# The first modulation by streamed matmuls and the norm chains by a power on GpSimd, in a two-layer diffusion trunk on one core

## Chip, core and metric

One core of one Trainium2 chip. The metric is device time in microseconds (us) of one execution of the program; lower is better. Engines are TensorE (PE; its weight loads are listed as PEld), VectorE (DVE), ScalarE (ACT), GpSimd (POOL) and SyncE (SP, which issues the DMA transfers).

## What is computed

Two token groups pass through two layers with shared weights: 128 context tokens and 512 latent tokens, width 1024, all in float32. Each layer is half an FFN, a mixer (layer 0: a Fourier mix, layer 1: attention), and half an FFN. Each of the three takes a normed input that is scaled and shifted by a modulation, and its output is normed, gated and added to the stream. Cut to what the change touches:

```python
def _rmsnorm(x, g):
    y = x * lax.rsqrt(jnp.mean(x * x, axis=-1, keepdims=True) + RMS_EPS)
    return y * g
def _modulation(cond, w_mod, b_mod):                  # 1024 -> 9 x 1024
    m = jax.nn.silu(cond) @ w_mod + b_mod
    return m.reshape(cond.shape[0], N_MOD, D_MODEL)
def _modulated_prenorm(x, g, m, k):
    return _rmsnorm(x, g) * (1 + m[:, 3 * k + 1, None]) + m[:, 3 * k, None]
def _half_ffn(x, m, k, g_pre, g_post, w1, w2):
    h = _modulated_prenorm(x, g_pre, m, k)
    return x + 0.5 * m[:, 3 * k + 2, None] * _rmsnorm(_swiglu(h, w1, w2), g_post)
# in reference(): m_ctx from c_ctx for context tokens, m_lat from c for latent tokens
```

## The kernel before

The stream lies transposed: channels in 8 chunks of 128 partitions, 640 tokens along the free dimension, in two halves of 320 (half 1 ends with the 128 context tokens). Every product of a weight block with a half is three matmuls of 320 columns (`mm3`, L209 to L211): high part of the weight with the high part of the input, high with low, low with high. So each weight unit of 128 x 1024 that SP loads into a `raw` tile is split once: ScalarE copies the high part (L192), another engine subtracts it for the low part (L194). That engine is VectorE, except for the units 2 to 7, which go to GpSimd. `split` (L203, L204) does the same with inputs.

The first FFN starts with the blocks f = 0 and 1 together (4 weight units), then 2, then 3, for half 0; then the same for half 1: 384 such matmuls, called products here. Then come blocks computed from combinations of both halves (`w1_fast`).

Modulations: a row of 128 outputs needs one tile of 512 KB. `gemv` (L349) multiplies it on VectorE with the conditioning vector, which `wide` holds on all partitions, and sums along the row, once for each of the two conditions. The first two modulations (`idx` 0 and 1, shift and scale of the first FFN) are needed before anything else. `begin` makes 12 of their 16 tiles so, first for the latent condition (L312), and after the first half's norm once more for the context condition (L328), and 4 tiles by matmuls with the weights as stationary operand (L308). The other modulations are `background` jobs: `behind` takes them one by one between matmuls.

Norm chains: `inverse_rms` adds up squares (L414), reduces over partitions by three one-column matmuls (L424), takes the root on ScalarE (L426) and the reciprocal on VectorE (L427), spreads the result to all partitions by three matmuls (L432) and copies it (L435). An early activation with a square root (L416) makes ScalarE change its function table in time. `pre` scales and splits the normed input, `post` gates the output and adds it to the stream. Both are generators: `tick` advances a clock by the matmuls written so far and takes the next step of a half's chain when its `yield` time is due. The matmuls of a chain are tied behind the latest product (`in_turn`), so they stand in TensorE's row among the products. There are 24 chains: two halves, two norms for each of six sub-layers. Within an engine the order is set when the program is built, by a scheduler that goes by dependencies and priority (`high_priority` moves work ahead).

In attention, `attend` lists for each block of 128 queries the steps scores, scale, transposes (`turn`, L1103, through one PSUM bank) and weighted sum (`take`, L1119), and `weave` drops them between the products at an even pace.

## Time and profile before

| | before |
|---|---|
| time, median of 3 runs | 2358.12 us (2357.97 to 2360.28) |
| profiled execution | 2358.87 us, span of its trace 2357.0 us |
| TensorE matmul busy | 2291.1 us (97%) |
| VectorE busy | 1718.2 us (73%) |
| ScalarE busy | 1313.8 us (56%) |
| GpSimd busy | 46.7 us (2%) |

The span runs from the first to the last instruction; 1.9 us of the profiled execution lie around it, and that execution stands 0.75 us above the median. Matmul ends are modelled, so a busy TensorE need not run at its peak; the number of matmuls in a stretch, against a stretch without waits, says how much it loses. An idle time is put down to the instruction that released the wait.

### The profile page before, as it was taken

How to read it: one execution, taken by the hardware profiler on the slowest of the kernel's cores; microseconds unless marked ns; L12 is line 12 of the kernel's file. 1: busy time of each engine (PE TensorE's matmuls, PEld its weight loads, DVE VectorE, ACT ScalarE, POOL GpSimd, SP SyncE). 2: the span in 40 equal slices, each digit the busy share in tenths (PEclk: the TensorE clock that was granted, in tenths of full speed). 3: DMA queues.
4: the chain of work that ended last, by engine and by line, in shares of the span. 5: the costliest groups of instructions: out<-in, count | busy, mean ns of one | idle time of the engine just before them, and what ended most of it. 6: DMA issues, size and time to landing. Idle time of an engine off the chain costs nothing.

```text
span 2357.0 us, 39382 instructions
## 1 busy us (share of the span) xinstructions
PE 2291.1 (97%) x15692; PEld 2244.9 (95%) x15692; DVE 1718.2 (73%) x2968; ACT 1313.8 (56%) x2524; POOL 46.7 (2%) x50
## 2 busy tenths in 40 slices
PE   6899999999999999999999999999999999999997
PEld 5899999998999999999999999988888999999997
DVE  7788788478888878855888877377877585755553
ACT  3445555574574545557545545576777774545545
POOL 3100000000000000000000000000000000000000
PEclk9999999999999999999999999999999999999999
DMA  7144344424424343451334433323543222321241
GB/s 261 47 139 147 109 131 129 151 93 126 152 81 143 118 128 122 144 170 54 117 109 143 144 123 127 117 89 120 160 143 116 75 89 72 99 90 59 85 135 45
DMA packets 80141, 277.10 MB, mean 118 GB/s; under 512 B 8786, under 2 KB 15186, under 8 KB 79956
## 3 DMA queue, kind: packets, MB, share of 16 engines
q1 hardware_dynamic: 79684, 274.25, 36.0%
q8 instruction: 123, 2.02, 0.4%
q14 instruction: 62, 0.51, 0.1%
q10 hardware_dynamic: 272, 0.33, 0.0%
HBM read 263.00 MB, written 11.53 MB: 116 GB/s over the span
## 4 chain that ended last, share of the span: by engine, by line
PE 86%; DVE 5%; ACT 4%; DMA 2%; issue 2%; POOL 0%; SPq 0%; ACTq 0%; DVEq 0%
PE main L209 25%; PE main L211 25%; PE main L210 25%; PE score L209 2%; PE score L210 2%; PE score L211 2%; DVE junk L349 2%; ACT hi L192 1%; PE sum L1119 1%; PE turn L1103 1%; PE score L1077 1%; DVE lo L194 1%; PE sum L424 1%; DMA raw<-in_w 1%; PE sum L432 1%
## 5 line engine op out<-in xcount | busy, mean ns | idle before, releaser
L209 PE MATMUL main<-ring,hi 128*128 128x320 f32 x3872 | 1203.2, 312 | 19.2 <-ACT ring L203 18.1
L210 PE MATMUL main<-ring,hi 128*128 128x320 f32 x3872 | 1201.5, 310 | 1.6 <-DVE ring L204 1.5
L211 PE MATMUL main<-ring,lo 128*128 128x320 f32 x3872 | 1200.8, 310 | 1.7 <-POOL lo L194 1.6
L209 PEld LDWEIGHTS main<-ring,hi 128*128 128x128 f32 x3872 | 728.3, 188 | 26.2 <-ACT ring L203 20.3
L210 PEld LDWEIGHTS main<-ring,hi 128*128 128x128 f32 x3872 | 730.1, 189 | 4.2 <-DVE ring L204 3.3
L211 PEld LDWEIGHTS main<-ring,lo 128*128 128x128 f32 x3872 | 729.5, 188 | 2.5 <-POOL lo L194 2.2
L192 ACT ACTIVATE hi<-raw 128x1024 fp32r<-128x1024 f32 (+1 forms) x358 | 350.7, 982 | 471.5 <-PE main L210 382.1
L194 DVE TENSOR_TENSOR lo<-raw,hi 128x1024 fp32r<-128x1024 f32 (+1 forms) x354 | 398.1, 1125 | 160.8 <-ACT hi L192 159.7
L349 DVE SCALAR_TENSOR_TENSOR junk<-raw,wide 128x1024 bf16<-128x1024 f32 x256 | 312.6, 1221 | 18.5 <-DMA raw<-in_w_mod_t 16.1
L644 ACT ACTIVATE y<-main 128x320 f32<-128x320 f32 x320 | 137.8, 432 | 170.4 <-PE main L211 169.2
L385 DVE TENSOR_TENSOR total<-total,square 128x640 f32<-128x640 f32 x71 | 58.3, 823 | 114.5 <-ACT square L384 113.6
L632 ACT ACTIVATE main<-y 128x320 f32<-128x320 f32 x256 | 111.8, 440 | 23.5 <-DVE left L618 9.9
L209 PE MATMUL score<-ring,hi 128*128 128x320 f32 x384 | 118.8, 310 | 0.9 <-ACT ring L203 0.9
L210 PE MATMUL score<-ring,hi 128*128 128x320 f32 x384 | 118.7, 309 | 0.4 <-DVE ring L204 0.4
L211 PE MATMUL score<-ring,lo 128*128 128x320 f32 x384 | 118.6, 309 | 0.0
L194 DVE TENSOR_TENSOR lo<-sums,hi 128x1024 fp32r<-128x1024 f32 x64 | 78.2, 1222 | 51.5 <-ACT hi L192 51.5
L211 PE MATMUL main<-ring,ring 128*128 128x320 f32 x352 | 110.0, 313 | 5.8 <-POOL ring L194 5.8
L209 PE MATMUL main<-ring,ring 128*128 128x320 f32 x352 | 111.5, 318 | 0.0
L210 PE MATMUL main<-ring,ring 128*128 128x320 f32 x352 | 109.8, 312 | 0.0
L192 ACT ACTIVATE hi<-sums 128x1024 fp32r<-128x1024 f32 x64 | 67.9, 1061 | 27.9 <-PE main L210 20.5
L203 ACT ACTIVATE ring<-right 128x320 fp32r<-128x320 f32 x112 | 51.6, 468 | 46.5 <-DVE right L531 38.0
L604 DVE TENSOR_TENSOR left<-left,main 128x320 f32<-128x320 f32 x64 | 31.2, 487 | 59.6 <-PE main L211 59.6
(189 smaller groups left out, 2783.4 us busy)
## 6 DMA issues: line engine op xcount, KB each, us to landing
raw<-in_w SPq DMA_DIRECT2D x264, 512.0 KB, 3.6
raw<-in_w_mod_t SPq DMA_DIRECT2D x128, 512.0 KB, 3.6
raw<-in_qkv SPq DMA_DIRECT2D x26, 512.0 KB, 3.6
spill<-ring SPq DMA_DIRECT2D x12, 640.0 KB, 3.4
ring<-spill SPq DMA_DIRECT2D x12, 640.0 KB, 5.4
raw<-in_bias SPq DMA_DIRECT2D x16, 448.0 KB, 3.6
first<-in_w_mod_t SPq DMA_DIRECT2D x8, 512.0 KB, 10.2
raw<-in_four_in SPq DMA_DIRECT2D x8, 512.0 KB, 3.6
```

The costliest lines, as they stand in the source:

```text
L192: nc.scalar.activation(hi, raw[:, at], AF.Copy)
L194: engine.tensor_tensor(lo, raw[:, at], hi.bitcast(F32), op=ALU.subtract)
L203: self.nc.scalar.activation(hi, src, AF.Copy)
L209: mm(out, whi, xhi, start=start, stop=False)
L210: mm(out, whi, xlo, start=False, stop=False)
L211: self.latest = mm(out, wlo, xhi, start=False, stop=stop)
L349: last = self.nc.vector.scalar_tensor_tensor(out=self.junk, in0=raw, scalar=1.0, in1=self.wide[:, cond, :], op0=ALU.mult, op1=ALU.mult, ac ...
L385: nc.vector.tensor_tensor(acc, acc, sq, op=ALU.add)
L424: nc.tensor.matmul(ps[:, j : j + 1], acc[0][:, t : t + P], self.ones[:, :1], start=True, stop=True)
L604: tt(a, q, z, op=ALU.subtract)
L632: nc.scalar.activation(ps[:, :HALF], self.y[:, m, lo:hi], AF.Copy)
L644: nc.scalar.activation(self.y[:, m, lo:hi], ps[:, :HALF], AF.Copy)
```

## The change

- `begin`: all 16 tiles of the first two modulations go through TensorE, with the conditions as stationary operand (32 columns, of which 2 are used) and the weights as moving operand: four matmuls of 256 columns a tile, each to its own 32 partitions of the output. The result is copied, turned by two small matmuls each, and copied to `mod`. Scale (`idx` 1) comes first, then x of half 0, then shift (`idx` 0). All `gemv` calls of `begin` go, for both conditions.
- `wide`, which the background jobs still need, is loaded by one broadcast DMA behind x of half 1 and run through Silu after the first FFN block.
- `send`: no low parts on GpSimd. `pre`: no products with the norm on GpSimd in the first chain.
- `inverse_rms`: instead of a square root and a reciprocal, VectorE adds EPS and GpSimd raises to the power -0.5; the early table change goes; the wait before the spread is 2200 instead of 1800. Parts of `pre`, `post` and the chain get high priority.
- `attend`: the scaling of the block before comes ahead of the new scores, and `take` is a step of its own.

```diff
@@ send
-        engine = nc.gpsimd if self.sent in range(2, 8) else nc.vector
-        engine.tensor_tensor(lo, raw[:, at], hi.bitcast(F32), op=ALU.subtract)
+        nc.vector.tensor_tensor(lo, raw[:, at], hi.bitcast(F32), op=ALU.subtract)
@@ setup
+        self.conds = self.temp("right")[:, : NCH * 32].rearrange("p (k m) -> p k m", m=32)
+        nc.scalar.activation(self.conds[:, :, :2], self.sk, AF.Silu)
@@ begin
+        for idx in (1, 0):
+            out = ps[:, idx * 256 : (idx + 1) * 256]
+            for k in range(NCH):
+                raw = self.wts.tile([P, UNIT], F32, tag=("hi", "lo")[k % 2], name=self.name("first"))
+                nc.sync.dma_start(out=raw, in_=io["w_mod_k"][idx, k])
+                for j in range(4):
+                    self.latest = nc.tensor.matmul(out[32 * j : 32 * j + 32], self.conds[:, k, :],
+                                                   raw[:, j * 256 : (j + 1) * 256], start=k == 0, stop=k == NCH - 1)
+                if idx == 0 and k in (4, 6):
+                    self.step(0)
+            with self.tc.high_priority():
+                rows = self.temp("left")[:, :256]
+                nc.scalar.activation(rows, out, AF.Copy)
+                turned = self.bank("score")[:, :16]
+                for a in range(2):
+                    nc.tensor.matmul(turned[:, a * 8 : a * 8 + 8].rearrange("p (j c) -> p j c", j=4),
+                                     rows[:, a * P : (a + 1) * P], sel, start=True, stop=True)
...
-        for raw, j in late:
-            with self.tc.issue_after(self.first_low.ins):
-                self.gemv(raw, 0, j, (1,))
+        nc.sync.dma_start(out=self.wide, in_=io["cond_rows"].unsqueeze(0).to_broadcast([P, 2, D]))
+        self.later = [partial(nc.scalar.activation, self.wide, self.wide, AF.Silu)]
@@ inverse_rms
-        nc.scalar.activation(self.col(1), acc[0][:, :1] if final else spare, AF.Sqrt)
...
-        nc.scalar.activation(col, ps[:, :3], AF.Sqrt, bias=self.eps, scale=1.0 / D)
-        nc.vector.reciprocal(col, col)
-        yield 1800
+        with high():
+            nc.vector.tensor_scalar_add(col, ps[:, :3], EPS)
+            nc.gpsimd.tensor_tensor(col, col, self.power, op=ALU.pow)
+        yield 2200
@@ pre
-            engine = nc.gpsimd if first and not half else nc.vector
-            engine.tensor_tensor(t, self.xpair(n, c, half), rb.to_broadcast([P, 2, HALF]), op=ALU.mult)
+            with high() if c == 0 else ExitStack():
+                nc.vector.tensor_tensor(t, self.xpair(n, c, half), rb.to_broadcast([P, 2, HALF]), op=ALU.mult)
@@ attend
+            if 1 <= n <= len(blocks):
+                parts.append(partial(scale, *blocks[n - 1]))
...
-            parts.append(lambda both=(before, after): [do() for do in both if do])
-            if before:
+            if n >= 2:
+                parts.append(partial(take, *blocks[n - 2]))
```

TensorE's row from the end of the modulations to the first products, before (L282 spreads the conditions, L308 is a modulation tile with stationary weights, L424 and L432 are the first norm chain, L209 to L211 the products):

```order
L282 MATMUL main_111<-ring_98,ones 128x512
L308 MATMUL turn_149<-sk,ring_150 128x2 x8
L424 MATMUL sum_136<-ones,total_122 128x1 x3
L432 MATMUL sum_143<-ident,col_140 128x128 x3
L308 MATMUL turn_149<-sk,ring_163 128x2 x8
L308 MATMUL turn_149<-sk,ring_173 128x2 x8
L308 MATMUL turn_149<-sk,ring_186 128x2 x8
L209 MATMUL main_318<-ring_234,hi_257 128x320
L210 MATMUL main_318<-ring_235,hi_257 128x320
L211 MATMUL main_318<-ring_234,lo_258 128x320
```

The same place now (L290 is a modulation tile in four column groups, L299 turns the result, L410 and L419 are the chain, L206 to L208 the products):

```order
L290 MATMUL turn_106<-first_206,right_98 32x256 x4
L410 MATMUL sum_212<-mean,total_170 128x1 x3
L290 MATMUL turn_106<-first_219,right_98 32x256 x4
L290 MATMUL turn_106<-first_225,right_98 32x256 x4
L419 MATMUL sum_231<-ident,col_216 128x128 x3
L290 MATMUL turn_106<-first_237,right_98 32x256 x4
L299 MATMUL score_245<-ident,left_243 128x8 x2
L206 MATMUL main_325<-ring_255,hi_278 128x320
L207 MATMUL main_325<-ring_256,hi_278 128x320
L208 MATMUL main_325<-ring_255,lo_279 128x320
```

The modulation now ends right ahead of the products in TensorE's own row, and the chain's spread stands ahead of its last tile.

VectorE's row around the first products, before (`ring_235` and `ring_247` are low parts of the input, `lo_258` and `lo_264` of the first weights, L349 the row sums):

```order
L349 SCALAR_TENSOR_TENSOR junk,mod<-ring_223,wide 128x1024
L316 COPY mod<-turn_149 128x4 x2
L364 TENSOR_TENSOR mod<-mod,vec 128x8
L366 SCALAR_TENSOR_TENSOR coef<-mod,vec 128x8
L462 TENSOR_SCALAR y<-y,coef 128x320 x4
L194 TENSOR_TENSOR lo_258<-raw_255,hi_257 128x1024
L204 TENSOR_TENSOR ring_235<-y,ring_234 128x640 x2
L349 SCALAR_TENSOR_TENSOR junk,mod<-first_160,wide 128x1024
L204 TENSOR_TENSOR ring_247<-y,ring_246 128x640 x2
L194 TENSOR_TENSOR lo_264<-raw_261,hi_263 128x1024
```

And now (L444 multiplies x with the norm, L349 is the coefficient, L450 scales, `ring_256` and `ring_268` are low parts of the input, `lo_279` and `lo_285` of the first weights):

```order
L444 TENSOR_TENSOR y<-ring_104,rms_235 128x2x320
L349 TENSOR_TENSOR coef<-mod,vec 128x8
L303 COPY mod<-score_245 128x8
L450 TENSOR_SCALAR y<-y,coef 128x320 x2
L349 TENSOR_TENSOR coef<-mod,vec 128x8
L450 TENSOR_SCALAR y<-y,coef 128x320
L444 TENSOR_TENSOR y<-ring_105,rms_235 128x2x320
L201 TENSOR_TENSOR ring_256<-y,ring_255 128x640 x2
L450 TENSOR_SCALAR y<-y,coef 128x320
L191 TENSOR_TENSOR lo_279<-raw_276,hi_278 128x1024
L201 TENSOR_TENSOR ring_268<-y,ring_267 128x640 x2
L191 TENSOR_TENSOR lo_285<-raw_282,hi_284 128x1024
```

The row sums between the splits are gone; two products of x with the norm, which stood on GpSimd, stand after the modulation's arrival.

VectorE's row at the chain of half 0 between the first FFN and the Fourier mix, before (L427 is the reciprocal, L456 the first work on the new input):

```order
L385 TENSOR_TENSOR total_4663<-total_4663,square_4750 128x640
L414 TENSOR_TENSOR total_4663<-total_4663 128x320
L385 TENSOR_TENSOR total_4725<-total_4725,square_4778 128x640
L427 RECIPROCAL col_4809<-col_4809 128x3
L385 TENSOR_TENSOR total_4725<-total_4725,square_4850 128x640
L194 TENSOR_TENSOR lo_4930<-raw_4927,hi_4929 128x1024
L456 TENSOR_TENSOR y<-ring_4362,rms_4831 128x2x320
```

And now (L413 adds EPS for GpSimd's power):

```order
L402 TENSOR_TENSOR total_4680<-total_4680 128x320
L191 TENSOR_TENSOR lo_4565<-raw_4562,hi_4564 128x1024
L413 TENSOR_SCALAR col_4814<-sum_4810 128x3
L372 TENSOR_TENSOR total_4729<-total_4729,square_4782 128x640
L191 TENSOR_TENSOR lo_4932<-raw_4929,hi_4931 128x1024
L444 TENSOR_TENSOR y<-ring_4368,rms_4839 128x2x320
```

The step on three columns keeps its place; a weight's low part stands right ahead of it, and two operations with two inputs right behind it, while GpSimd works. In TensorE's row 15 products stand between sum and spread of this chain now, where 21 stood.

## Rows read from the trace of the kernel before

**Rows 1.** From the profile's page, part 1: busy time of each engine in us, its share of the span, and its instructions.

```profile
PE 2291.1 (97%) x15692; PEld 2244.9 (95%) x15692; DVE 1718.2 (73%) x2968; ACT 1313.8 (56%) x2524; POOL 46.7 (2%) x50
```

**Rows 2.** Busy time by stretches: the first FFN's 384 products, a stretch of the same length without waits behind it, and two of three alike stretches at the end of an FFN or mixer. Columns: stretch, its length, busy us and number of instructions of TensorE, its weight loads, VectorE, ScalarE and GpSimd, then the granted clock of TensorE, the share of the DMA engines, GB/s.

```profile
38.50:118.00 79.50, 67.45 (x396) 65.30 (x397) 63.78 (x91) 35.44 (x61) 20.78 (x6) 0.91 0.20 62
118.00:197.50 79.50, 79.50 (x545) 79.50 (x544) 65.92 (x104) 35.35 (x58) 0.00 (x0) 1.00 0.42 132
494.00:506.00 12.00, 9.70 (x66) 8.86 (x65) 8.51 (x15) 11.36 (x25) 0.00 (x0) 1.00 0.32 104
...
1544.00:1556.00 12.00, 9.76 (x65) 9.18 (x64) 8.51 (x15) 11.38 (x24) 0.00 (x0) 0.95 0.47 141
```

**Rows 3.** Who waited for whom on TensorE over the whole span: the waiting tile and line, the one that released it, then us in total, times, longest.

```profile
PE main L209 <- ACT ring L203: 18.1, 5, 10.5
...
PE main L211 <- POOL ring L194: 5.8, 1, 5.8
...
PE sum L424 <- DVE total L414: 4.9, 2, 2.7
...
PE turn L1103 <- ACT right L1105: 4.5, 11, 0.8
```

**Rows 4.** Instructions in order of time up to the first products: start us, us, engine, line, operation, tiles, shape, number, and in brackets the idle time before it and what ended it.

```profile
2.25 1.96 SPq L294 DMA_DIRECT2D ring<-in_x  x4
...
3.74 0.33 PEld L282 LDWEIGHTS main<-ring,ones 1*128 1x128 f32 x1 [0.52 <-issue]
...
4.59 0.33 PEld L282 LDWEIGHTS main<-ring,ones 1*128 1x128 f32 x1 [0.53 <-issue]
...
14.36 1.42 PE L424 MATMUL sum<-ones,total 128*128 128x1 f32 x6
...
31.31 1.06 ACT L192 ACTIVATE hi<-raw 128x1024 fp32r<-128x1024 f32 x1 [12.79 <-DMA raw<-in_w]
...
36.45 0.17 DVE L366 SCALAR_TENSOR_TENSOR coef<-mod,vec 128x8 f32<-128x8 f32 x1
36.73 1.51 DVE L462 TENSOR_SCALAR y<-y,coef 128x320 f32<-128x320 f32 x4
38.16 1.22 DVE L194 TENSOR_TENSOR lo<-raw,hi 128x1024 fp32r<-128x1024 f32 x1
39.29 1.55 DVE L204 TENSOR_TENSOR ring<-y,ring 128x640 fp32r<-128x640 f32 x2
...
40.16 1.36 ACT L203 ACTIVATE ring<-y 128x640 fp32r<-128x640 f32 x2
...
40.60 0.47 PE L211 MATMUL main<-ring,lo 128*128 128x320 f32 x1
...
43.80 0.47 PE L211 MATMUL main<-ring,lo 128*128 128x320 f32 x1
```

**Rows 5.** Stretches at the lower clock, columns as in rows 2: two in the first FFN, and the two right behind the ends of sub-layers near 1108 and 1555 us.

```profile
56.40:63.20 6.80, 4.72 (x21) 4.75 (x21) 6.02 (x7) 0.72 (x2) 3.95 (x2) 0.50 0.47 140
82.00:94.00 12.00, 6.21 (x25) 5.94 (x24) 3.88 (x7) 0.38 (x1) 6.08 (x1) 0.72 0.14 44
1107.70:1111.10 3.40, 3.40 (x14) 3.40 (x14) 3.40 (x6) 3.40 (x9) 0.00 (x0) 0.50 0.00 0
1554.90:1558.30 3.40, 3.40 (x15) 3.40 (x14) 3.40 (x6) 3.40 (x9) 0.00 (x0) 0.50 0.57 214
```

**Rows 6.** TensorE in order of time in attention, where two query halves are written to two column groups (128*64 is the stationary tile).

```profile
1628.23 0.32 PE L1119 MATMUL sum<-right,total 128*64 128x128 f32 x1
1628.24 0.32 PE L1119 MATMUL sum<-right,ring 128*64 128x128 f32 x1
1628.39 0.27 PE L1119 MATMUL sum<-right,total 128*64 128x128 f32 x1
```

**Rows 7.** GpSimd's instructions with two inputs, and one of VectorE in the time of the third; columns as in rows 4.

```profile
18.61 10.02 POOL L456 TENSOR_TENSOR y<-ring,rms 128x640 f32<-128x640 f32 x4 [17.30 <-ACT rms L435]
...
59.61 2.36 POOL L194 TENSOR_TENSOR lo<-raw,hi 128x1024 fp32r<-128x1024 f32 x1 [1.63 <-DVE junk L349]
...
81.08 7.00 POOL L194 TENSOR_TENSOR ring<-raw,ring 128x1024 fp32r<-128x1024 f32 x1 [13.71 <-ACT ring L192]
...
85.06 0.82 DVE L577 TENSOR_TENSOR total<-y 128x640 f32<-128x640 f32 x1
...
1652.39 0.45 POOL L928 TENSOR_TENSOR ring<-ring,ring 64x128 fp32r<-64x128 f32 x1 [19.29 <-ACT ring L927]
```

**Rows 8.** From the profile's page, part 5: groups of VectorE's instructions by line: number, busy us and mean ns of one, idle time of the engine just before them and what ended most of it.

```profile
L194 DVE TENSOR_TENSOR lo<-raw,hi 128x1024 fp32r<-128x1024 f32 (+1 forms) x354 | 398.1, 1125 | 160.8 <-ACT hi L192 159.7
L349 DVE SCALAR_TENSOR_TENSOR junk<-raw,wide 128x1024 bf16<-128x1024 f32 x256 | 312.6, 1221 | 18.5 <-DMA raw<-in_w_mod_t 16.1
```

**Rows 9.** The norm chain of half 0 at the end of the first FFN, columns as in rows 4; the last row is the first product that waits behind it.

```profile
494.12 1.28 ACT L416 ACT_TABLE_LOAD   x1
495.41 0.20 ACT L416 ACTIVATE col<-total 128x1 f32<-128x1 f32 x1
...
497.84 0.24 ACT L426 ACTIVATE col<-sum,eps 128x3 f32<-128x3 f32 x1
...
498.12 0.18 DVE L427 RECIPROCAL col<-col 128x3 f32<-128x3 f32 x1 [2.92 <-ACT col L426]
...
504.81 0.85 PE L209 MATMUL main<-ring,hi 128*128 128x320 f32 x4 [2.24 <-ACT ring L203]
```

More of the change, by code (lines that the diff above doesn't have):

```diff
@@ L279, in setup @@
-        for cond, r in enumerate((rows, more)):
-            for a in (0, 512):
-                ps = self.bank()
-                nc.tensor.matmul(ps, self.ones[:1, :], r[:1, a : a + 512], start=True, stop=True)
-                nc.scalar.activation(self.wide[:, cond, a : a + 512], ps, AF.Silu)
     def begin(self):
         nc, io = self.nc, self.io
-        late = []
-        order = [("t", f) for f in range(NCH)] + [("t", NCH + f) for f in range(PE_MOD, NCH)]
-        for f, n in enumerate(PE_AT):
-            order.insert(n, ("k", f))
@@ L292, in begin @@
         self.new_x(0)
-        for c in range(0, NCH, 2):
-            nc.sync.dma_start(out=self.xpair(0, c, 0), in_=io["x"][:, c : c + 2, :HALF])
-        self.launch(0, self.pre(0, 0, 0), 0)
-        for _ in range(3):
-            self.step(0)
-        ps = self.bank("turn")
-        for n, (kind, j) in enumerate(order):
-            if kind == "k" or len(late) >= 8:
-                raw = self.ring(F32)[:, :UNIT]
-            else:
-                raw = self.wts.tile([P, UNIT], F32, tag=("hi", "lo")[len(late) % 2], name=self.name("first"))
-            if kind == "k":
-                nc.sync.dma_start(out=raw, in_=io["w_mod_k"][j])
-                with self.tc.issue_after(self.spread.ins) if j > 1 else ExitStack():
-                    for k in range(NCH):
-                        nc.tensor.matmul(ps[:, 2 * j : 2 * j + 2], raw[:, k * P : (k + 1) * P], self.sk[:, k, :],
-                                         start=k == 0, stop=k == NCH - 1)
-            else:
-                nc.sync.dma_start(out=raw, in_=io["w_mod_t"][0, j])
-                last = self.gemv(raw, 0, j, (0,))
-                late.append((raw, j))
@@ L434, in inverse_rms @@
         r = self.temp("rms")[:, :HALF]
-        nc.scalar.activation(r, ps[:, :HALF], AF.Copy)
+        with high():
+            nc.scalar.activation(r, ps[:, :HALF], AF.Copy)
         if final:
@@ L443, in pre @@
         nc = self.nc
-        first = acc is None
         n = layer * 3 + sub
@@ L478, in post @@
         for c in range(0, NCH, 2):
-            t = self.pair(self.y, c, half)
-            engine, rb = (nc.gpsimd, r) if final and c == 2 else (nc.vector, rp)
-            engine.tensor_tensor(t, t, rb[:, :HALF].unsqueeze(1).to_broadcast([P, 2, HALF]), op=ALU.mult)
-            x = self.xpair(layer * 3 + sub + 1, c, half)
-            engine.tensor_tensor(x, x, t, op=ALU.add)
-            if last:
-                queue = nc.scalar if final and c == 2 else nc.sync
-                queue.dma_start(out=self.io["x_out"][:, c : c + 2, lo:hi], in_=x)
-            else:
-                acc = self.sum_square(acc, x)
+            with self.tc.high_priority() if c == NCH - 2 else ExitStack():
+                t = self.pair(self.y, c, half)
+                engine, rb = (nc.gpsimd, r) if final and c == 2 else (nc.vector, rp)
+                engine.tensor_tensor(t, t, rb[:, :HALF].unsqueeze(1).to_broadcast([P, 2, HALF]), op=ALU.mult)
+                x = self.xpair(layer * 3 + sub + 1, c, half)
+                engine.tensor_tensor(x, x, t, op=ALU.add)
+                if last:
+                    queue = nc.scalar if final and c == 2 else nc.sync
+                    queue.dma_start(out=self.io["x_out"][:, c : c + 2, lo:hi], in_=x)
+                else:
+                    acc = self.sum_square(acc, x)
             yield 2500
@@ L532, in w1 @@
                     hidden(f, v, half)
+                while self.later:
+                    self.later.pop()()
         def late(f, j, half):
@@ L1134, in attend @@
                 parts += [partial(ctx_scores if b == "c" else scores, c, b, p0) for p0 in range(2)]
[L1135 to L1138 removed]
+            if n >= 2:
+                parts.append(partial(take, *blocks[n - 2]))
+            if 1 <= n <= len(blocks):
                 parts += [partial(turn, *blocks[n - 1], p0) for p0 in range(2)]
```

67 lines of the change are left out of this document (31 added, 36 removed).

## The prediction

> **What bounds the kernel now.** The page's busy times come first: TensorE is the bound (97%), VectorE has a quarter of its time free, ScalarE nearly half, GpSimd does next to nothing [rows 1]. But a busy share hides what a matmul costs while it waits inside or runs slowly, so the second view is matmuls by stretch. Undisturbed, 545 stand in 79.50 us, 0.1459 us each; the first FFN has 396 in as long a stretch, 149 too few, or 21.7 us lost [rows 2]. At the ends of sub-layers 65 to 66 stand where 82 would, 2.4 us lost each [rows 2]. The third view, who waits for whom, names them: 18.1 us for the first input parts on ScalarE, 5.8 us in one wait for a low part on GpSimd, 4.9 us at the sums of squares, 4.5 us in small pieces in attention [rows 3]. So what can move the time is the start, three boundaries and attention; a cheaper VectorE or ScalarE elsewhere is worth nothing.
>
> **The start.** The third product begins at 40.60 [rows 4].
>
> *When the last modulation tile lands.* The weights of the first product arrive at 31.31, when ScalarE begins to split them [rows 4]. They and all 16 modulation tiles are one queue, and the same bytes stand ahead of the last tile after the change. From the first load at 2.25 to 31.31 about 10.2 MB pass, so a tile of 512 KB takes 1.5 us and the last of them lands at 31.31 - 1.5 = 29.8.
>
> *Its matmuls.* No row shows a moving weight tile of 256 columns. The spreading of the conditions has 512 columns a pass and float32 takes two passes; its passes begin 0.855 apart (3.74 and 4.59, [rows 4]), so two passes of 256 columns cost 0.855 at that pace. If the four column groups run side by side, a tile costs about 0.9, less than the 1.5 at which tiles land; if they run one after another, 3.4. The nearest row is attention's pair into two column groups: they begin 0.01 apart, and the next pair 0.15 later [rows 6]. I take side by side. All tiles done: 29.8 + 0.9 = 30.7.
>
> *From there to the coefficients.* ScalarE's copy of 256 columns 0.4 (640 columns take 0.68 [rows 4]); two turns in float32 0.9 (three small matmuls take 1.42 [rows 4]); a copy 0.1; a product of x with the norm that stands ahead on VectorE 0.8 (two inputs, 640 columns, as a low part of the input, 1.55 for two [rows 4]); the coefficient 0.2 [rows 4]. That is 33.1, with hops between engines 33.4. Before, it was 36.6 [rows 4].
>
> *VectorE to the first low weight part.* In its row stand two more copies and coefficients 0.3, three scalings at 0.38, a product 0.8, two input lows 1.55 and the low weight 1.22 [rows 4]: 5.0. The third product needs that: 38.4, against 40.60. Gain 2.2.
>
> *The 384 products.* 381 more at 0.1459 are 55.6. Three surcharges remain. The first products stand 0.267 apart ((43.80 - 40.60)/12 [rows 4]), 320 columns at 1.2 GHz, for some 6 us: 2.8. The second half's norm chain has 12 small passes, 1.5. Its spread now stands three products behind the sum, so I let it wait 1.0. End at 38.4 + 55.6 + 5.3 = 99.3, against 118.0 [rows 2]. **Gain 18.7.** Counted the other way, from what goes: the stretch with the wait for GpSimd's low part (5.8 [rows 3]) and the lower clock around it, 25 matmuls in 12 us where 82 fit, loses 8.3; the one at 0.50, 21 matmuls in 6.8 us where 47 fit, 3.8 [rows 5]; the shorter of the two waits at the sums 4.9 - 2.7 = 2.2 [rows 3]; the earlier start 2.2: 16.5. The other 2 would be short waits that I have not traced one by one. VectorE covers it: it loses 24 row sums of the first modulations at 1.22 (29.3 [rows 8]) and gains six low parts (7.3) and four products (3.2). In its new order all that stands ahead of the last low part of these blocks sums to 25 us from the first products, so it would be through at 64, where TensorE asks for it at 68. The cover is 5 us thick; without it the surplus would show as waits. Between 14 and 21 I put the start's gain.
>
> **The boundaries.** There TensorE waits on the chain spread, then norm copy, product, scaling and input high, and the first product of the next sub-layer starts 2.24 late behind ScalarE's input part [rows 9]. The change lets the spread stand some 18 products (2.65 us) earlier relative to that product, which covers 2.24; the y product gets priority. Twice a slow stretch follows, 14 matmuls in 3.40 us where 23 fit, clock at 0.50 [rows 5], 1.3 to 1.7 lost; it starts right behind the idle time, and goes if the idle time goes. Best 3 x 2.4 + 2 x 1.7 = 10.6, worst 0; I take **7**, since in 2.65 against 2.24 a hop of 0.4 decides.
>
> **The chains.** 24 of them. Out: ScalarE's root 0.24 and VectorE's reciprocal 0.18 [rows 9]. In: an add on VectorE 0.18 and a power on GpSimd. No row shows a power. The smallest two-input operation of GpSimd, 64 x 128, takes 0.45 [rows 7]; the largest, 128 x 1024, 2.36, and 7.00 where VectorE worked on two inputs at the same time, [rows 7] shows one of these operations at 85.06. I take 0.45 since the power has three columns; the ends are 0.2 and 7.0. Mostly 15 products, 2.2 us, stand between sum and spread now, so copy-in, add, power and hops of 1.3 keep a slack of 0.9. A few chains have 0 to 9 products there (at the start and in the last sub-layers): I give back **2**, between 0 and 6. The early activation and its table load, 1.28 and 0.20 [rows 9], leave ScalarE, which is covered everywhere; priced at nothing, since ScalarE's part of the boundary comes after it.
>
> At the table load the trace shows no cost beside its own: it ends at 495.40, and the next activation starts at 495.41 [rows 9]. The Trainium skill, "ScalarE: Activation LUTs", section "What ACT_TABLE_LOAD costs", adds a drain of about 1380 ns to every switch. By that rule each boundary would lose 1.4 us more of ScalarE, and the change would come out some 4 us better, at about 2329; by the row it is nothing, and the row decides.
>
> **Attention and the end.** The waits of the transposes for ScalarE's copies sum to 4.5 [rows 3]. The scaling comes earlier and the weighted sum is a step of its own, which may take some away or put other waits there: -4 to +3, I take a gain of **1**. The end, 0.
>
> **The sum.** 2358.87 (profiled execution) - 18.7 - 7 + 2 - 1 = 2334.2. That execution stands 0.75 above the median of the runs: **2333**.
>
> **Rivals.**
>
> *The boundaries keep their wait.* The next link behind the spread (rms copy, product, scaling, split) is as long as before, and if it had been held by VectorE's queue and not by the spread, the 7 do not come: 2340. For it: VectorE is busy 8.51 of 12 us there [rows 2]; against: the wait ends with ScalarE's input part [rows 3].
>
> *The column groups do not run side by side.* Then 16 tiles at 3.4 take 55 us at the low pace, and the start would be lost altogether (2363), or, at full clock, 1.7 a tile, a few tenths slower than they land, and the first products come some 6 us later: 2339. For it: moving weights into four groups are in no row; against: the pairs [rows 6].
>
> *The first power is late.* The first chain's spread stands ahead of the last modulation tile in TensorE's row. If GpSimd needs 6 us longer for its first power, the spread comes at about 32.6 and holds the last tile's matmuls; that is 3.5 to 4 us: 2337. Against: GpSimd's first two-input operation starts at 18.61 behind the norm's copy, with nothing between [rows 7]; but that is another operation.
> The Trainium skill, "GPSIMD Engine Reference", section "2.1 Instruction dispatch", states such a delay: the first call of a freshly loaded kernel pays about 6 us with no instruction in the profile to show for it. No row of the trace before can show whether a power is one.
>
> *Slower: every chain waits for the power.* The chains' spread stands in TensorE's row, so a late power stops all products. If GpSimd's small operation is stretched by VectorE's two-input work as the large one was (7.00 against 2.36, [rows 7]), or the power itself is long, 23 chains pay. At 0.45 + 4.6 less the slack of 0.9 it is 4.2 each, 96 us: about 2430. It decides from (25.7 + 4.7)/23 = 1.3 us a chain, a power of some 2.2 us. For it: the row at 81.08, and that two operations with two inputs stand behind the add in VectorE's row; against: the operation at 64 x 128 took 0.45 in attention, with VectorE at work.
>
> *The start's gain is half given back.* The products then catch up with VectorE's low parts, whose cover is only 5 us: 2343 to 2352.
>
> **How the numbers follow.** Forecast 0.55; boundaries 0.15; column groups 0.08; first power 0.07; slower 0.10; half given back 0.05. Low ends: start 21, boundaries 10.6, chains 0, attention 3 give 2324, one beyond is 2322. High ends: start 14, boundaries 3, chains 5, attention 0 give 2346, and 2348 takes in most of the rivals but the slow one. Range 2322 to 2348. A measurement of this kernel can tell about 0.2%, 4.7 us, from no change. Slower: the fourth rival, 0.09 of its 0.10; same: 0.05, the rest of it and the ends of the second and fifth; faster 0.86.
>
> **What would show it.** First products at 35 to 39, no wait for a low part, no stretch at 0.50 between 56 and 94, the 384th product at 99. Modulation matmuls four at a time, 0.9 a tile. Boundary stretches with 75 to 82 matmuls in 12 us. GpSimd's power under 1 us, and TensorE's waits at the spread of a few us in all; were they 30, the fourth rival holds. Wrong it would be also if a wait for low parts on VectorE appears in the first FFN, or if the first products start at 40 or later.

## The result and the profile after

The changed kernel takes 2336.14 us (median of 4 runs, 2334.20 to 2337.46) against 2359.20 for the kernel before (four runs; the 2358.12 further up is the median of the first three): ratio 0.9901, with a 95% interval of 0.9886 to 0.9917. The forecast was 2333 in a range of 2322 to 2348. The profiled execution took 2334.20, its span 2332.4, 24.6 us shorter than before.

The page's busy times come first, to be laid beside [rows 1].

```profile
PE 2278.2 (98%) x15756; PEld 2225.2 (95%) x15756; DVE 1686.6 (72%) x2934; ACT 1270.9 (54%) x2448; POOL 45.4 (2%) x64
```

They say little: TensorE is at 98% where it was at 97%. The stretches say where the time came from. Columns as in [rows 2]: the first FFN, and the ends of the three sub-layers that lost 2.4 us each before.

```profile
38.50:118.00 79.50, 77.50 (x519) 77.23 (x520) 64.00 (x99) 41.53 (x67) 1.81 (x1) 0.98 0.32 102
...
476.00:488.00 12.00, 12.00 (x85) 12.00 (x84) 11.31 (x18) 11.82 (x27) 0.39 (x1) 1.00 0.32 105
1078.00:1090.00 12.00, 12.00 (x84) 11.77 (x83) 10.20 (x18) 11.85 (x26) 0.86 (x1) 1.00 0.14 45
1520.00:1532.00 12.00, 12.00 (x85) 11.90 (x83) 10.68 (x16) 11.81 (x27) 0.46 (x1) 1.00 0.57 175
```

The first stretch holds 519 matmuls where 396 stood, and the ends of sub-layers hold 84 or 85 in 12 us where 65 or 66 stood: TensorE no longer stops there.

A better measure than any stretch is the same product in both traces. Both kernels issue 14,400 products; the start of one before, less the start of the same one now, is the time gained up to there (us):

```
products gone by               start before   gained   gained in this piece
0 (first FFN begins)               38.59       2.78     +2.8
384 (its first blocks are done)   118.14      18.41    +15.6
2,950 (near the FFN's end)        497.84      17.86     -0.6
3,000 (Fourier mix has begun)     508.75      21.44     +3.6
3,250                             550.18      22.27     +0.8
4,000 (mix is over)               686.86      20.02     -2.3
6,800 (near the 2nd FFN's end)   1101.84      20.46     +0.4
7,000                            1138.24      23.86     +3.4
9,760 (near the 3rd FFN's end)   1546.71      23.61     -0.3
9,800                            1556.51      27.55     +3.9
10,000 (attention runs)          1592.10      25.34     -2.2
11,200 (end of attention)        1864.57      25.81     +0.5
14,399 (the last one)            2342.17      25.48     -0.3
```

So the start gave 18.4, the three boundaries 3.6 + 3.4 + 3.9 = 10.9, and 2.3 and 2.2 of it were lost again, in the Fourier mix and where attention begins. Behind the last product 0.9 more went.

The waits of TensorE (columns as in [rows 3]) name what is left.

```profile
PE turn L290 <- DMA first<-in_w_mod_k: 9.9, 12, 5.7
PE main L208 <- DVE ring L201: 8.0, 6, 1.9
PE turn L1092 <- ACT right L1094: 5.0, 11, 1.2
PE sum L419 <- POOL col L414: 4.6, 6, 1.6
PE sum L410 <- DVE total L402: 4.5, 1, 4.5
PE main L206 <- ACT ring L200: 2.9, 1, 2.9
```

The waits for ScalarE's input part, 18.1 before, are 2.9, and the one for GpSimd's low part is gone. Of the 18.1, 10.5 stood ahead of the first product, which comes only 2.8 earlier; in their place stand the modulation's matmuls and their waits for tiles (9.9, of which 5.7 ahead of the first one). New is 4.6 for GpSimd's power. The 8.0 for low input parts are the Fourier mix, the 4.5 the beginning of attention.

The start in order of time (TensorE, then GpSimd and VectorE; columns as in [rows 4]):

```profile
24.55 1.08 PE L290 MATMUL turn<-first,right 128*32 128x256 f32 x8 [0.20 <-DMA first<-in_w_mod_k]
...
26.93 2.24 PE L290 MATMUL turn<-first,right 128*32 128x256 f32 x16
...
27.28 0.86 POOL L414 TENSOR_TENSOR col<-col,power 128x3 f32<-128x3 f32 x1 [25.98 <-DVE col L413]
...
29.10 1.65 PE L419 MATMUL sum<-ident,col 128*128 128x128 f32 x6
...
30.68 1.08 PE L290 MATMUL turn<-first,right 128*32 128x256 f32 x8
...
34.65 0.16 DVE L349 TENSOR_TENSOR coef<-mod,vec 128x8 f32<-128x8 f32 x1
...
35.80 0.63 PE L206 MATMUL main<-ring,hi 128*128 128x320 f32 x1 [2.92 <-ACT ring L200]
...
38.91 0.63 PE L208 MATMUL main<-ring,lo 128*128 128x320 f32 x1 [1.59 <-DVE lo L191]
```

A tile's eight passes go in two fours; a four starts within 0.02 us and the second 0.43 behind the first, so by its starts a tile is through in about 0.85 (the row's 1.08 has the modelled end of the last in it), and TensorE waits for the next to land, every 1.28 us. The chain's spread (29.10) stands ahead of the last tile and holds it until 30.68. The third product starts at 38.91, against 40.60.

### The profile page after: what moved, and what is told of

Read it like the earlier page. It is cut to its first block, busy times and chain, and to the rows that moved or that the text cites. A ratio compares the mean times of both kernels' runs of the same rounds, so it can differ in the third digit from the quotient of the medians.

```text
span 2332.4 us, 39397 instructions
## 1 busy us (share of the span) xinstructions
PE 2278.2 (98%) x15756; PEld 2225.2 (95%) x15756; DVE 1686.6 (72%) x2934; ACT 1270.9 (54%) x2448; POOL 45.4 (2%) x64
## 4 chain that ended last, share of the span: by engine, by line
PE 88%; DVE 5%; ACT 3%; DMA 3%; issue 1%; POOL 0%; SPq 0%; DVEq 0%; ACTq 0%; POOLq 0%
PE main L206 25%; PE main L208 25%; PE main L207 25%; PE score L206 3%; PE score L208 3%; PE score L207 3%; DVE junk L336 1%; PE sum L1108 1%; PE turn L1092 1%; PE sum L419 1%; DVE lo L191 1%; ACT hi L190 1%; PE score L1066 1%; DMA first<-in_w_mod_k 1%; DMA raw<-in_w_mod_t 1%
## 5 line engine op out<-in xcount | busy, mean ns | idle before, releaser
L206 PE MATMUL main<-ring,hi 128*128 128x320 f32 x3872 | 1204.5, 312 | 3.9 <-ACT ring L200 2.9
L208 PE MATMUL main<-ring,lo 128*128 128x320 f32 x3872 | 1198.0, 310 | 1.6 <-DVE lo L191 1.6
L206 PEld LDWEIGHTS main<-ring,hi 128*128 128x128 f32 x3872 | 727.7, 188 | 10.0 <-ACT ring L200 3.8
L208 PEld LDWEIGHTS main<-ring,lo 128*128 128x128 f32 x3872 | 727.6, 188 | 2.2 <-DVE lo L191 1.9
L621 ACT ACTIVATE main<-y 128x320 f32<-128x320 f32 x256 | 111.9, 439 | 27.2 <-DVE left L607 10.5
L206 PE MATMUL score<-ring,hi 128*128 128x320 f32 x384 | 118.8, 309 | 0.0
L208 PE MATMUL score<-ring,lo 128*128 128x320 f32 x384 | 118.7, 309 | 0.0
L206 PE MATMUL main<-ring,ring 128*128 128x320 f32 x352 | 110.5, 315 | 0.0
L208 PE MATMUL main<-ring,ring 128*128 128x320 f32 x352 | 108.9, 309 | 0.0
```

The lines of the kernel that those rows point to most:

```text
L206: mm(out, whi, xhi, start=start, stop=False)
L208: self.latest = mm(out, wlo, xhi, start=False, stop=stop)
L621: nc.scalar.activation(ps[:, :HALF], self.y[:, m, lo:hi], AF.Copy)
```

## The experiments

The distances in this section are gained time against the kernel before, product by product as in the table. One limit on them: kernels with the same start (the changed one and the one with the old order of attention) had gained 18.4 and 16.3 at product 384, in one profile each. The modulation tiles landed 0.3 to 1.3 us later in the second. So a difference of 2 us in the start says nothing.

### What gave the start its 18 us

Two edits could: the row sums leave VectorE, and the low parts leave GpSimd. Each was made alone.

```diff
@@ send, in the changed kernel
-        nc.vector.tensor_tensor(lo, raw[:, at], hi.bitcast(F32), op=ALU.subtract)
+        engine = nc.gpsimd if self.sent in range(2, 8) else nc.vector
+        engine.tensor_tensor(lo, raw[:, at], hi.bitcast(F32), op=ALU.subtract)
```

> The changed kernel, with the low parts of units 2 to 7 back on GpSimd and nothing else. Theory A: the start's 18.4 us come from VectorE, which no longer has the row sums of the modulations between the low parts; then GpSimd has little two-input work of VectorE beside it, its low parts take 2.4 us each instead of 7.0, and the time stays within 3 us of the changed kernel's 2336. Theory B: the low parts on GpSimd were the cost; then the wait of 5.8 us and the slow-clock stretches come back, 10 to 14 us: 2346 to 2350.

Measured: 2339.55 (2337.84 to 2341.24), 0.991 of before; gained at product 384: 12.9. Its waits and two of GpSimd's rows:

```profile
PE main L209 <- POOL ring L192: 2.3, 1, 2.3
PE main L209 <- POOL lo L192: 1.9, 2, 1.6
```

```profile
57.71 3.00 POOL L192 TENSOR_TENSOR ring<-raw,ring 128x1024 fp32r<-128x1024 f32 x1
69.45 2.75 POOL L192 TENSOR_TENSOR ring<-raw,ring 128x1024 fp32r<-128x1024 f32 x1 [8.73 <-ACT ring L190]
```

The other half, in the kernel before:

```diff
@@ send, in the kernel before
-        engine = nc.gpsimd if self.sent in range(2, 8) else nc.vector
+        engine = nc.vector
```

> The kernel before, with the low parts of units 2 to 7 on VectorE and nothing else. Theory A (VectorE's row sums are the cost): VectorE gets 7.3 us more on top of 29 us of row sums in the same stretch, the waits only change their name, 2357 to 2366. Theory B (GpSimd's low parts are the cost): 10 to 14 us better, 2345 to 2349.

Measured: 2348.46 (2345.79 to 2349.32), 0.9947; gained at product 384: 11.9. So, gained at product 384:

```
                              row sums on VectorE   modulation on TensorE
low parts 2 to 7 on GpSimd            0                    12.9
low parts 2 to 7 on VectorE          11.9                  18.4
```

The second column is the changed kernel's whole start: its third product also comes 1.3 and 1.7 us earlier.

Neither theory holds in both runs. In the first, theory A misses its 3 us by 0.4 (2339.55 against 2336.14) and B by more than 6; in the second, B's range holds and A's does not. Either edit alone takes away some 12 us, the second adds 5.5 or 6.5.

The rows show that GpSimd's low parts and VectorE's work with two inputs hold each other up, and that VectorE was held first. In the kernel before (GpSimd, VectorE and TensorE; the first and second VectorE rows stand beside the low parts at 51.85 and 54.65):

```profile
52.38 3.38 DVE L349 SCALAR_TENSOR_TENSOR junk<-first,wide 128x1024 bf16<-128x1024 f32 x1
...
54.65 3.34 POOL L194 TENSOR_TENSOR ring<-raw,ring 128x1024 fp32r<-128x1024 f32 x1
...
55.70 2.64 DVE L414 TENSOR_TENSOR total<-total 128x320 f32<-128x320 f32 x1
...
58.48 1.41 PE L424 MATMUL sum<-ones,total 128*128 128x1 f32 x6 [2.17 <-DVE total L414]
...
72.57 1.22 DVE L349 SCALAR_TENSOR_TENSOR junk<-ring,wide 128x1024 bf16<-128x1024 f32 x1
```

The first five low parts on GpSimd took 2.36 to 3.34, and beside each of them one instruction of VectorE was held: four row sums (2.74 to 3.46 where one alone takes 1.21) and the sum of squares at 55.70 (2.64; the second run has it at 60.09 with 0.48). Together that is 10.3 us of VectorE's time, and TensorE waited 2.2 for that sum of squares. The sixth low part, the 7.00 of [rows 7], is another case: it began at 81.08, 7 us behind the end of the last row sum (72.57), beside VectorE's splits, sums and squares with two inputs, and ended 2.2 after the last of these. In the first run, without row sums, the same low part took 2.75 at 69.45, and it was VectorE that was held: its square at 69.92 took 2.96, and 0.82 in the kernel before. How much of the gain each of these holds is worth, no run takes apart. That VectorE had room for the low parts even with the row sums (theory A said it had not) shows in the second run, which waits for no low part of a weight in this stretch.

### Whether the column groups matter

```diff
@@ begin
-                    ... matmul(out[32 * j : 32 * j + 32], ..., start=k == 0, stop=k == NCH - 1)
+                    ... matmul(out[:32], ..., start=k == 0 and j == 0, stop=k == NCH - 1 and j == 3)
```

> The changed kernel with the four matmuls of a modulation tile written to the same 32 partitions, all accumulating in one sum; the modulations of the first FFN's input are therefore other numbers, and the time alone counts. If the four column groups ran side by side, a tile now takes 8 passes of 0.43 us, 3.4 us against 1.3 us at which tiles land; 16 tiles end at about 5.7 + 55 = 61 where they ended at 31.8: the whole 29 us slower less what of the start still hides, 2358 to 2366. If they did not run side by side already: 2334 to 2340.

The copy behind it now takes 32 partitions, and VectorE fills the rest with zeros.

Measured (one run): 2333.38, where the kernel before took 2360.09. Neither expectation holds as written. TensorE's modulation rows:

```profile
5.50 15.27 PE L290 MATMUL turn<-first,right 128*32 128x256 f32 x64 [5.50 <-DMA first<-in_w_mod_k]
...
21.83 8.82 PE L290 MATMUL turn<-first,right 128*32 128x256 f32 x40
```

The time was the same, but for another reason than "not side by side". In one group the passes start 0.427 apart for the first six and 0.216 apart from then on (40 passes in 8.82 us are 0.22 each), 1.2 and then 2.4 GHz; the first record of the granted clock in this trace is 1.00 at 8.13, where the pace doubles. In four groups the second four stayed 0.43 behind the first up to the last tile: 1.2 GHz. There the granted clock has no record before 32.02, so the level is read from the pace, and a second row agrees: the spread's six passes took 1.65 at 29.10 and 0.83 at 477.40. A tile in one group takes 1.73 us, half of the 3.4 that I had worked out at the low pace. The first product came 5.9 us later (41.69 against 35.80), as the prediction's rival had it for that case; but the low part of the first weight was ready by then (third product 3.2 later), and at product 384 only 1.6 was left of it, within the scatter of the start.

### What closed the boundaries

Power or priority? Each was undone alone, then both.

```diff
@@ inverse_rms, first run (root)
-            nc.vector.tensor_scalar_add(col, ps[:, :3], EPS)
-            nc.gpsimd.tensor_tensor(col, col, self.power, op=ALU.pow)
+            nc.scalar.activation(col, ps[:, :3], AF.Sqrt, bias=self.eps, scale=1.0)
+            nc.vector.reciprocal(col, col)
@@ and the early activation ahead of the sum, as before
@@ inverse_rms and pre, second run (no priority)
-        high = self.tc.high_priority
+        high = ExitStack
@@ post, second run
-            with self.tc.high_priority() if c == NCH - 2 else ExitStack():
+            with ExitStack():
```

> The changed kernel, with the root on ScalarE, the reciprocal on VectorE and the early activation as before; priorities, the later due time of the spread and all else as changed. Theory P: the power closes the three boundaries (10.6 us measured there, some 4 given back later); then they open again, 2342 to 2348, with 65 to 70 matmuls in 12 us instead of 82 to 84. Theory H: the priority of the chain and of the first products with the norm closes them; then 2335 to 2339.

Measured: 2335.05 (2333.27 to 2337.58), 0.9893 of before.

> The changed kernel without the high priority in the chains, in the first product with the norm and in the last step of the gating; the power stays. Theory P: 2335 to 2339, boundaries stay closed. Theory H: boundaries open, 2342 to 2348.

Measured: 2334.88 (2334.52 to 2335.47), 0.9892 of before. Neither run opened the boundaries: over the three places of the table the first gains 3.2, 4.0 and 3.6, the second 2.7, 3.2 and 3.1, beside 3.6, 3.4 and 3.9 in the changed kernel. Theories P and H each fall as the only cause. Both undone:

> The changed kernel with both undone: the root on ScalarE and the reciprocal on VectorE as before, and no high priority in chain, first product with the norm and gating; the due time of the spread stays changed. Theory E (either one suffices, since each takes the chain past the work queued on ScalarE): the spread stands 34 products behind the sum at the first boundary again, and the boundaries lose 2.4 us and the slow-clock stretches behind them as before, 9 to 11 us less at the three places, of which some 4 were given back later anyway: 2341 to 2348. Rival (a third edit, the due time or the attention steps, closed them): 2334 to 2339, the shift against the kernel before grows by 9 us or more over the three boundaries.

Measured: 2341.89 (2341.48 to 2342.74), 0.9925. The first two of the three boundaries are open again (the third stands later than the stretch shown above):

```profile
476.00:488.00 12.00, 9.41 (x61) 8.74 (x60) 8.43 (x15) 11.53 (x25) 0.00 (x0) 0.97 0.26 88
...
1078.00:1090.00 12.00, 10.60 (x75) 10.20 (x73) 7.08 (x11) 11.51 (x27) 0.00 (x0) 1.00 0.30 103
```

From product 2,950 to 3,000, 6,800 to 7,000 and 9,760 to 9,800 this run gains -1.9, 0.0 and -0.5 against before, where the changed kernel gains 3.6, 3.4 and 3.9. TensorE and ScalarE at the first chain show why (the sum, the early table load, four gates, the root, the spread and the first product behind them):

```profile
474.01 0.72 PE L412 MATMUL sum<-mean,total 128*128 128x1 f32 x6
...
475.58 1.28 ACT L406 ACT_TABLE_LOAD   x1
...
477.85 1.38 ACT L392 ACTIVATE y<-y,coef 128x192 f32<-128x192 f32 x4
...
479.13 0.25 ACT L415 ACTIVATE col<-sum,eps 128x3 f32<-128x3 f32 x1
...
479.73 0.91 PE L421 MATMUL sum<-ident,col 128*128 128x128 f32 x6
...
486.03 0.86 PE L206 MATMUL main<-ring,hi 128*128 128x320 f32 x4 [2.47 <-ACT ring L200]
```

The sum is ready at 474.73, and the root begins at 479.13: for 4.4 us it stands in ScalarE's row behind a gate, a square, the early table load with its activation (1.5 us together), a copy that waits 0.4 for TensorE, and four more gates. The spread stands 34 products behind the sum, as theory E had it. The same chain in the changed kernel:

```profile
474.54 0.72 PE L410 MATMUL sum<-mean,total 128*128 128x1 f32 x6
...
475.30 0.16 DVE L413 TENSOR_SCALAR col<-sum 128x3 f32<-128x3 f32 x1
...
475.54 0.85 POOL L414 TENSOR_TENSOR col<-col,power 128x3 f32<-128x3 f32 x1 [16.98 <-DVE col L413]
...
477.40 0.83 PE L419 MATMUL sum<-ident,col 128*128 128x128 f32 x6
```

Here 2.9 us pass from sum to spread, there 5.7. Priority brings the root forward in ScalarE's row; the power goes round that row. With the root and priority, ScalarE's row is:

```profile
474.14 1.28 ACT L415 ACT_TABLE_LOAD   x1
475.43 0.26 ACT L415 ACTIVATE col<-sum,eps 128x3 f32<-128x3 f32 x1
```

The root waits there for a table load of its own, begins 1.2 us behind the sum (474.19), and the boundary stays closed. Either one does it, and theory E holds. Which of the priorities (chain, first product with the norm, last gating) is the one that counts, no run separates.

### What a longer power would cost

```diff
@@ inverse_rms
             nc.gpsimd.tensor_tensor(col, col, self.power, op=ALU.pow)
+            nc.gpsimd.tensor_tensor(col, col, self.once, op=ALU.pow)     # exponent 1
```

> The changed kernel with a second power (exponent 1, the same result) behind the first on GpSimd in each of the 24 chains. It adds 0.85 to 1.8 us to each chain. If the slack is what the prediction worked out (0.9, now 0.5 since the power takes 0.86 and not 0.45), most chains wait, 0.3 to 1.3 us each: 8 to 20 us, 2344 to 2356, and TensorE's waits for GpSimd at the spread go from 4.6 to 12 us or more. If the chains have more room than that: below 5 us, 2336 to 2341.

Measured: 2353.23 (2352.06 to 2353.99), 0.9971: 17 us of the 23 are gone again. Its wait at the spread:

```profile
PE sum L422 <- POOL col L417: 19.1, 17, 2.6
```

17 of the 24 chains wait, 19.1 in all, where 6 waited 4.6. At the last product this run is 18.3 behind the changed kernel, 0.76 a chain; 3.3 of it stand by product 384 already, where two chains lie and the start scatters. The rival "every chain waits for the power" is real, and one power more reaches it.

### Where the 2.3 us in the Fourier mix went

VectorE was busy 30.29 of 32 us there in the changed kernel, TensorE 28.08 (the line from 569.00 below; columns as in [rows 2]). So the mix runs at VectorE's pace, and TensorE's being early is waited away. A stretch of the mix in the kernel before looks the same, VectorE at 30.79 of 32 us:

```profile
588.00:620.00 32.00, 28.42 (x184) 27.63 (x183) 30.79 (x64) 17.10 (x31) 0.00 (x0) 0.89 0.55 174
```

Moving 14 background modulation jobs, 28 row sums, to the first FFN should show it.

```diff
-BEHIND = (28, 20, 28, 28, 24, 0)
+BEHIND = (42, 20, 28, 28, 24, 0)
@@ fourier
-                self.behind(2)
...
-            if g < 6:
-                self.behind()
```

> The changed kernel with the 14 background modulation jobs of the Fourier mix moved to the first FFN (42 jobs there in place of 28). Theory V: 10.4 us are lost between 550 and 600 us because VectorE is the bound there, with 14 jobs of two row sums (1.22 us each, 34 us) between the folds and splits; they go, and TensorE loses 2 to 4 there; the first FFN's VectorE has the room: 2326 to 2331. Rival: the jobs only cause waits earlier, in the first FFN: 2334 to 2340.

Measured: 2323.15 (2321.82 to 2323.38), 0.9843 of before, 13 us better than the changed kernel (11 by the two profiled executions). The same stretch in the changed kernel, and then in this one:

```profile
569.00:601.00 32.00, 28.08 (x182) 27.59 (x183) 30.29 (x61) 14.71 (x26) 0.00 (x0) 0.89 0.57 185
```

```profile
569.00:601.00 32.00, 32.00 (x223) 31.85 (x223) 20.12 (x40) 15.63 (x29) 0.00 (x0) 1.00 0.41 132
```

From product 3,000 to 4,000 the run gains 10.0 where the changed kernel loses 1.4, and the first FFN shows no new wait: from product 384 to 2,800 the gained time moves by 0.2 in both. The same edit in the kernel before:

> The kernel before with the 14 modulation jobs of the Fourier mix moved to the first FFN, as in the run that moved them in the changed kernel. Theory V (VectorE was the bound of the Fourier mix before too, so a start of the mix that is 4 us earlier was partly waited away there, 1.9 us): 8 to 11 us better than before, 2348 to 2352, and the changed kernel with the jobs moved stays 25 to 28 us ahead of it, where changed and before are 23 apart. Rival (the change itself made VectorE the bound there): less than 5 us better, 2355 to 2360.

Measured: 2347.26 (2346.35 to 2348.58), 0.9944. Theory V holds in its first part: 13.4 better, more than the 8 to 11. The second part fails: the two kernels with moved jobs are 24.1 apart, not 25 to 28. Product by product, the 1.4 that the changed kernel loses from 3,000 to 4,000 is down to 0.3 (20.38 ahead at the one, 20.04 at the other), but the run in the changed kernel had 1.8 less from its start, within the scatter, and the one before gained 1.5 at the second boundary by itself.

### The order in attention

Scaling and weighted sum were put back as one step behind the scores (the last part of the diff, undone).

> The changed kernel with attention's steps in the order before (scaling and weighted sum as one step behind the scores). The prediction gave the new order 1 us, between -4 and +3; in the traces the distance to the kernel before grows by 0.5 us between the first and the last block of attention. If the new order does that: 2336 to 2338, with the transposes' waits for ScalarE 0 to 2 us longer in sum. If the new order costs time (the 2.2 us lost where attention begins): 2332 to 2335.

Measured: 2336.95 (2335.53 to 2337.68), 0.99. From product 10,000 to 11,200 it loses 0.4 where the changed kernel gains 0.5: by these two profiles the new order is worth 0.9; the medians, 0.8 apart, lie within the scatter of the runs. From 9,940 to 10,000 both lose 0.7, and from 9,800 to 9,940 both lose 1.5, so that loss is not the new order's.

### The fastest, without the power

> The changed kernel with the jobs of the Fourier mix in the first FFN and, in place of the power, the root on ScalarE and the reciprocal on VectorE at high priority. If the power is worth nothing beside the priority: as with the power, 2321 to 2325. If the power still carries something once the Fourier mix has room: 2326 to 2330.

Measured: 2324.24 (2323.25 to 2326.61), 0.9848, beside 0.9843 (0.9829 to 0.9858) with the power: no difference that these runs can tell. Both moved-job kernels beat the changed one.

## Why the prediction held, point by point

**The start** (forecast 18.7, measured 18.4). The steps came out close, some by errors that cancel. The last tile landed about on time, but the spread ahead of it held it by 1.3, so the coefficients came at 34.8 and not 33.4. VectorE then needed 4.1 to the low weight and not 5.0, and the third product started at 38.91 (forecast 38.4). The half-speed products ended at 42.3 and not after 6 us; the second chain cost 3.2 beyond its share and not 2.5. The 384th product ended near 99.7 (forecast 99.3). The cover of VectorE, 5 us, held: no wait for a low weight after 38.91. My account of what went, wait by wait, was weaker than it looked: the wait of 2.2 at the sum ends at 58.48 and lies inside the stretch from 56.40 to 63.20 that I had priced at 3.8, so it is counted twice, and 14.3 and not 16.5 of the 18.4 are named. The experiments add that its items are not separate: the low parts on GpSimd and the row sums, each taken away alone, give 11.9 and 12.9, and together not 24.8 but 18.4. The earlier third product alone is 1.7.

**The boundaries** (forecast 7 of at most 10.6, measured 10.9). The step was right: the spread stands 17 products earlier (2,937 against 2,954) with the first product of the mix at 2,976 in both, and the wait and the slow stretches behind it went. The term was taken too small because I feared a hop. I had put it down to the chain as a whole; that the ScalarE queue, not the table load or the root's 0.24, was the obstacle, is what the three runs showed.

**The give-back**, 2.3 + 2.2, was in no term. The first is shown above to be VectorE's pace in the mix, and with it falls a sentence of the prediction, that a cheaper VectorE elsewhere is worth nothing: moving 28 row sums out of the mix was worth 13 us in either kernel. The second is only argued: where attention begins, the second half's sum waits 4.5 for VectorE (2.7 before), whose row is busy 19.92 of 20.60 us ahead of it and was 16.65 of 20.60 at that place before.

```profile
1533.00:1553.60 20.60, 16.24 (x121) 16.03 (x120) 19.92 (x32) 12.19 (x26) 4.22 (x5) 1.00 0.22 66
```

TensorE came earlier, VectorE's work of gating did not get shorter. No run took that work away. With it the forecast's 7 for the boundaries and the 6.4 that was left after both come close, which is chance.

**The chains** (forecast -2). The waits at the spread are 4.6, of which 1.6 lie in the start, but the run with the root, which has none of them on GpSimd, is as fast: 25.5 gained at the last product in both. So the power costs nothing over a root with priority and brings nothing. The size of the power was wrong: I took 0.45; it is 0.85 in 14 chains and 1.23 to 1.89 in 10. The slack of 0.9 beyond 0.45 was of the right order: the second power ends 1.1 behind the first on average and costs 0.76 a chain, so some 0.4 was left beyond the first.

**Attention** (forecast +1, measured +0.9). The number came out, the reason did not: the transposes' waits for ScalarE, from which I took the term, are 5.0 now, 4.5 before and 4.6 with the old order. **The end** (forecast 0, measured -0.9): 0.3 of it lies between the last sum and its spread, where TensorE waits 1.2 for the power, the rest behind the spread; why is open.

**The rivals.** Boundaries keep their wait: no. Column groups: they do run side by side; the rival's price of 6 us was right for the first product and wrong for the end, since most of it is won back by product 384. The first power late: no, 0.86, as later ones; the Trainium skill, "GPSIMD Engine Reference", section "2.1 Instruction dispatch", states some 6 us for the first call of a freshly loaded kernel, and this trace shows none for this operation. Table loads: 30 became 3, and with 34 in the run with the root the time is the same. The drain that the Trainium skill, "ScalarE: Activation LUTs", section "What ACT_TABLE_LOAD costs", adds to each switch does not show: in all three traces ScalarE was idle for at most 0.02 us ahead of each load but the first, and in all but six cases the next activation began 0.01 behind the load. The 4 us that I worked out from it did not show either. Slower: one power away, see above. The start's gain half given back: no, 17.9 of the 18.4 still stood at product 2,950.

## What to carry to other kernels

A small operation on a chain can wait far longer in an engine's row than it takes: look where it stands among that engine's work, and either move it ahead or send it round by an engine that is idle. Once TensorE's waits go in one place, expect part of the gain back wherever another engine sets the pace; the busy shares of the stretch tell it beforehand (here VectorE at 30.8 of 32 us in the Fourier mix of the kernel before), and moving optional work out of that stretch, 14 jobs here, was worth 13 us in either kernel, over half of what the whole change brought. Two partners that hold each other up, here GpSimd and VectorE on two-input work, should be costed together; either edit alone gave two thirds of the start's gain.

## What the hardware showed that I had not expected

Small matmuls in four column groups left TensorE at its lower clock: four passes of 256 columns start within 0.02 us and the next four 0.43 later, up to the last tile at 30.68, while the same passes one after another went from 0.427 to 0.216 apart after six. TensorE was idle for some 0.2 us ahead of most tiles in the first case and not at all in the second up to 20.77. Side by side is 4 times the work per time at the low clock (3.4 us a tile against 0.85), but only 1.73 / 0.85 = 2.0 times against the full one.

A power of 128 x 3 on GpSimd takes 0.85 us, and up to 1.89 when VectorE is already at work on two inputs. Two cases of the changed kernel, GpSimd's rows and then VectorE's:

```profile
475.54 0.85 POOL L414 TENSOR_TENSOR col<-col,power 128x3 f32<-128x3 f32 x1 [16.98 <-DVE col L413]
...
1879.72 1.89 POOL L414 TENSOR_TENSOR col<-col,power 128x3 f32<-128x3 f32 x1 [11.51 <-DVE col L413]
```

```profile
476.14 0.82 DVE L372 TENSOR_TENSOR total<-total,square 128x640 f32<-128x640 f32 x1 [0.68 <-ACT square L371]
...
1879.68 1.23 DVE L191 TENSOR_TENSOR ring<-raw,ring 128x1024 fp32r<-128x1024 f32 x1
```

In the first, VectorE was idle for 0.60 us of the 0.85; in the second a low part had begun 0.04 before the power. So it is with all 24: ahead of each of the ten slow powers an operation of VectorE with two inputs had begun, 0.04 to 0.22 us before, and the power ended 0.70 us behind the end of that operation; ahead of the 14 of 0.85 none had, and one of them, at 1533.08, kept its 0.85 though a low part began 0.03 behind it. Here who started first decided. The Trainium skill, "GPSIMD Engine Reference", section "1. Specifications", says that GpSimd's access to SBUF is shared with VectorE and that VectorE's instructions with two inputs there contend with it; the 24 powers agree.
